# Last two expert steps: first weights ahead of the second weights, and a combine between the last sums

## The chip, the cores and the metric

The kernel runs on one core of a Trainium2 chip. The metric is the device time of one execution in microseconds (us); lower is better. The time before is the median of three runs, and one further execution was taken with the hardware profiler on.

## What is computed

The reference is a two-layer transformer block on 256 tokens of width 1024, all in fp32. Each layer has four kinds of attention with gates (the token mixers), a layer norm, then a grouped mixture of experts and a second layer norm. Only the mixture of experts is touched here:

```python
N_EXPERTS = 32; N_GROUPS = 8; TOP_K = 2; D_EXPERT = 256

def grouped_moe(x, w_router, router_bias, w1, w3, w2):
    ...  # one group of 4 experts per token, the best two experts in it, gates that sum to 1
    def expert_block(args):
        xb, e = args
        hid = jax.nn.silu(xb @ w1[e]) * (xb @ w3[e])
        return hid @ w2[e]
    ...
    y = jnp.zeros((t, d), x.dtype).at[tok].add(ys[dest] * gate_sorted[:, None])

for l in range(DEPTH):
    ...
    ffn = grouped_moe(x, w_router, router_bias, moe_w1[l], moe_w3[l], moe_w2[l])
    x = layer_norm(DN_ALPHA * x + ffn, ln2_g[l], ln2_b[l])
```

Per layer an expert has 1024x256 floats of `w1`, as many of `w3` ("first weights", 2 MB in all) and 256x1024 floats of `w2` ("second weights", 1 MB). With 32 experts that is 96 MB per layer, every byte of which is read once.

## The kernel before

Each layer first runs the mixers (projections, attention, gates, `w_out`), then routes the tokens, then works through the experts in a loop over `q` from 0 to 7 (L1535). A step `q` takes four experts: `2q`, `2q+1` and the same plus 16. Steps 0 to 5 pass two experts at a time through the array, with up to 64 tokens for each. The last two steps, 6 and 7 (`QUADS`, L43), put all four experts side by side as column tiles of 32 tokens.

What a step of the last two issues on TensorE, in this order:

- `head4` (L1385): for each of 8 slices `j` of the contraction and for each of the four experts `t`, one product with the first weights of 512 columns (L1390). One such product is two MATMUL instructions in the trace. The four experts lie in different columns of the array and run together where their data is there together.
- `combine` of the step before (L1480): the one-hot matrix `oht` times the step's gated outputs `ys`, added into the four accumulators `acc`; 8 matmuls (L1488).
- `flip_key` (L1462) for the one-hot matrix of this step, then `flip` (L1405), which transposes the hidden values into `hT`. ScalarE copies `hT` out of PSUM (L1410).
- `tail` (L1419): 16 products with the second weights (L1440), by halves `c` of the contraction and halves `fh` of the output columns. With four experts the order is `c`=0 for both `fh`, then `c`=1 for both. After `c`=1 of an `fh`, `evac` (L1424) takes the sum out: ScalarE L1430, then VectorE L1431.

After step 7 the last `combine` follows, then the statistics and the layer norm (`stats` L1635, `norm2` L1647). In layer 0 they lead into the next layer, in layer 1 to the output. In layer 1 `norm2` first loads its gain and offset, 512 KB each, into two of the four `b4` buffers (L1664); these are the buffers of step 6's `ys`, and so they come free with the combine of step 6.

TensorE's order is the order in which the code is written (`manual_schedule`, L1528); the other engines' orders follow from it through tile buffers and priorities.

The weights come by one queue, SyncE's, in the order of the list `loads` (L1048). A load of first weights (`load_head`, L1018) is two transfers of 512 KB for one expert's four slices of `w1` and `w3`; with four experts, all slices 0 to 3 come first, then all slices 4 to 7. A load of second weights is one transfer of 1 MB (`load_out`, L1025), and in step 7 two of 512 KB by `c`, all `c`=0 first (`load_out4`, L1039). Each transfer on the queue waits until the one eight places ahead of it has landed, since eight semaphores go round.

Weights land in 20 buffers of 1 MB (`SLOTS`, L41), taken in turn by `mslot` (L995). A buffer is free again when the products that read its contents 20 loads earlier have run. `release` (L1067) sets how many loads the program issues ahead.

`keep_warm` (L304) issues n fp32 products of 128x256 on the identity (L308), whose results nobody reads.

Of the kernel before, what the change touches and what calls it, by code (L numbers as in the profile page):

```python
# [10 lines left out]
F32 = mybir.dt.float32  # L11
# [35 lines left out]
NW3 = 5  # L47
NE_ = 4
# [54 lines left out]
def build(ctx, tc, I, consts, out, dbg=None, layers=L):  # L103
# [270 lines left out]
    for l in range(layers):  # L374
# [24 lines left out]
        with ExitStack() as mst:  # L399
# [649 lines left out]
            for q in range(NQ):  # L1049
                for s in range(2):  # L1050
                    a13s[q, s], a2s[q, s] = [{}, {}], [[], []]
                    if q not in QUADS:
                        loads += [partial(load_head, q, s, h) for h in range(4)]
                if q in QUADS:
                    loads += [partial(load_head, q, s, h) for h0 in (0, 2) for h in (h0, h0 + 1) for s in range(2)]
                if q == NQ - 1:
                    loads += [partial(load_out4, q, c, s, i) for c in range(2) for s in range(2) for i in range(2)]
                else:
                    loads += [partial(load_out, q, s, i) for s in range(2) for i in range(2) if q or s]

# [6 lines left out]
            def release(n):  # L1067
                cnt[1] += n
                load_ahead(cnt[1] + len(SLOTS))
# [271 lines left out]
        with ExitStack() as ost:  # L1341
# [77 lines left out]
            def tail(passes, gcol, out, final=None, between=None):  # L1419
# [14 lines left out]
                for s, (hT, tiles) in enumerate(passes):  # L1434
                    end = s == len(passes) - 1
                    four = len(tiles) == 4
                    for a, b in ((0, 0), (0, 1), (1, 0), (1, 1)):
                        fh, c = (b, a) if four else (a, b)
                        for r0, n, a2 in tiles:
                            pe.matmul(pys[fh][r0:r0 + n, :], hT[:, c, r0:r0 + n], a2[c][:, fh * 512:fh * 512 + 512],  # L1440
                                      start=(s == 0 and c == 0), stop=(end and c == 1), skip_group_check=True,
                                      tile_position=(0, r0) if four else None)
# [82 lines left out]

            xgs = {0: a8((8, G))}
            prev = None
            with tc.manual_schedule(engines={mybir.EngineType.PE}):  # L1528
# [6 lines left out]
                for q in range(NQ):  # L1535
                    b, o = q // 2, q % 2 * 128
                    more = b + 1 < NQ // 2
                    ths = []
                    if q in QUADS:
                        a13q = [a13s.pop((q, s)) for s in range(2)]  # L1540
                        ph = head4(lambda j, t: xgs[b][:, j, o + 32 * t:o + 32 * t + 32],
                                   [a13q[t % 2][t // 2] for t in range(4)])
                        release(8)
                        with behind_counts(q):
                            ths.append(hidden(ph, misc(6)))
                    for s in range(2) if q not in QUADS else ():
                        if q == 0 and s:
                            for tb in range(2):
                                pe.transpose(pkt[0:NP, tb, :], keyP[:, tb, :], ident)
                            act.activation(keyT[0:NP], pkt[0:NP], AF.Copy)  # L1550
                        ph = head(lambda j, i: xgs[b][:, j, o + 64 * i:o + 64 * i + 64], a13s.pop((q, s)),
                                  None if q or s else ph0)
                        release(3 if q == 1 and s == 0 else 4)
                        with behind_counts(q):
                            ths.append(hidden(ph, mk[:, s, q:q + 1]))
                    if o and more:
                        xgs[b + 1] = a8((8, G))
                    if prev is not None:
                        combine(*prev, first=q == 1)
# [9 lines left out]
                    hTs = [flip(th) for th in ths]  # L1569
                    if o and more:  # L1570
                        gather(xgs[b + 1], ohs[b + 1], G)
                    final = q == NQ - 1
# [6 lines left out]
                    else:  # L1579
                        passes = [(hT, pair_tiles(a2)) for hT, a2 in zip(hTs, a2q)]  # L1580
                    ys = tail(passes, gcols[q % 2], partial(b4, (2, 512)),
                              final, next_pieces if final and l + 1 < layers else None)
# [155 lines left out]
```

## Time and profile before

| What | Value |
|---|---|
| time before, median of 3 runs | 985.3 us (981.02 to 986.99) |
| profiled execution, its own time | 982.18 us |
| its span, first to last instruction | 980.4 us |
| mean granted TensorE clock | 0.987 of full speed |
| TensorE busy | 937.5 us (96%) |
| VectorE, ScalarE, GpSimdE busy | 489.1 (50%), 400.3 (41%), 199.4 us (20%) |
| SyncE's transfers | 282.48 MB, 77.9% of the DMA engines' time |
| last two steps of layer 0, of layer 1 | about 441 to 483 us, about 924 to 966 us |

All stretches below are microseconds from the start of the profiled span. The span lies inside the execution's own time; 1.8 us lie around it. The 77.9% are an average: in the expert loops of both layers the DMA engines are full, in the mixers they are not.

### The profile page before, as it was taken

Reading aid. Unit: us, or ns where it says so; the run is one execution under the profiler, and the core shown is the slowest. Engines: PE = TensorE matmul, PEld = TensorE weight load, DVE = VectorE, ACT = ScalarE, POOL = GpSimd, SP = SyncE. Lnnn points to the kernel's source line nnn. Section 1 sums busy time; section 2 is a strip of 40 time slices with the busy share of each in tenths; the row PEclk is TensorE's granted clock in tenths of the full one; section 3 lists DMA queues with packets and bytes.
Section 4 is the critical chain, followed back from the end, with each engine's and each line's share of the span. In section 5 each row is a group of like instructions: output and inputs, shape, how many; then the busy total and the mean of one; then the engine's idle time right before and its main releaser. Section 6 shows DMA issues by size and latency. Waiting matters only on the chain.

```text
span 980.4 us, 16559 instructions
## 1 busy us (share of the span) xinstructions
PE 937.5 (96%) x6335; PEld 668.1 (68%) x6335; DVE 489.1 (50%) x1158; ACT 400.3 (41%) x856; POOL 199.4 (20%) x190
## 2 busy tenths in 40 slices
PE   8999999999999999998799999999999999999964
PEld 7989999999953434342397999989999443343421
DVE  4776767766661212121277666686686521121214
ACT  4755666665431212120164766666654111121101
POOL 5440123122020313100045201140220203130001
PEclk9999999999999999999999999999999999999998
DMA  9795454469779999999998444534897899999994
GB/s 283 238 282 169 132 173 130 152 230 413 294 259 392 407 414 412 414 408 407 370 289 246 132 146 154 172 130 164 292 410 251 285 416 409 410 408 414 407 408 188
DMA packets 122585, 287.08 MB, mean 293 GB/s; under 512 B 10526, under 2 KB 73764, under 8 KB 115844
## 3 DMA queue, kind: packets, MB, share of 16 engines
q1 hardware_dynamic: 121092, 282.48, 77.9%
q0 software_dynamic: 1264, 3.41, 1.6%
q8 instruction: 52, 0.85, 0.4%
q14 instruction: 33, 0.27, 0.1%
q10 hardware_dynamic: 144, 0.07, 0.0%
HBM read 284.55 MB, written 1.38 MB: 292 GB/s over the span
## 4 chain that ended last, share of the span: by engine, by line
PE 63%; DMA 19%; issue 9%; DVE 6%; ACT 2%; POOL 0%; SPq 0%; POOLq 0%; ACTq 0%; DVEq 0%
PE pj L466 13%; PE pj L468 12%; PE pj L467 12%; DMA w<-in_moe_w 10%; PE h L1381 9%; DMA xw<-in_moe_w 7%; PE y L1440 4%; PE po L601 2%; PE at L613 2%; DMA w<-in_w_in 2%; PE tp L592 1%; PE at L308 1%; DVE b L421 1%; PE acc L1488 1%; DVE big L1215 1%
## 5 line engine op out<-in xcount | busy, mean ns | idle before, releaser
L421 DVE TENSOR_TENSOR b<-w,b 128x512 fp32r<-128x512 f32 (+2 forms) x294 | 212.2, 737 | 102.4 <-ACT b L416 98.1
L416 ACT ACTIVATE b<-w 128x512 fp32r<-128x512 f32 (+2 forms) x294 | 179.8, 623 | 130.5 <-PE pj L468 103.4
L466 PE MATMUL pj<-big,b 128*128 128x256 f32 x736 | 214.8, 292 | 1.7 <-ACT b L416 0.7
L468 PE MATMUL pj<-big,b 128*128 128x256 f32 x736 | 210.1, 285 | 1.5 <-DVE b L421 1.5
L467 PE MATMUL pj<-big,b 128*128 128x256 f32 x736 | 209.9, 285 | 0.0
L466 PEld LDWEIGHTS pj<-big,b 128*128 128x128 f32 x736 | 142.5, 194 | 8.2 <-issue 4.1
L468 PEld LDWEIGHTS pj<-big,b 128*128 128x128 f32 x736 | 142.6, 194 | 2.6 <-DVE b L421 2.1
L467 PEld LDWEIGHTS pj<-big,b 128*128 128x128 f32 x736 | 142.8, 194 | 0.1
L1401 DVE SCALAR_TENSOR_TENSOR th<-th,h 128x256 f32<-128x256 f32 x28 | 11.8, 420 | 178.2 <-ACT th L1400 178.2
L1381 PE MATMUL h<-xw,a 128*64 128x512 f32 x384 | 99.0, 594 | 0.1
L1400 ACT ACTIVATE th<-h 128x256 f32<-128x256 f32 x28 | 10.7, 383 | 204.8 <-PE h L1381 152.7
L1381 PE MATMUL h<-w,a 128*64 128x512 f32 x272 | 84.2, 593 | 0.0
L1431 DVE SCALAR_TENSOR_TENSOR b<-y,gcol,b 128x512 fp32r<-128x512 f32 x30 | 22.5, 751 | 100.6 <-ACT b L1430 93.7
L1440 PE MATMUL y<-w,hT 128*64 128x512 f32 (+1 forms) x256 | 66.2, 595 | 3.0 <-ACT hT L1410 2.8
L1381 PEld LDWEIGHTS h<-xw,a 128*64 128x64 f32 x384 | 31.4, 137 | 53.4 <-issue 49.3
L561 POOL TENSOR_TENSOR R<-R,a 128x512 f32<-128x512 f32 x20 | 35.3, 1776 | 111.9 <-DVE a L556 106.3
L466 PE MATMUL pj<-b,big 128*128 128x256 f32 x192 | 55.9, 291 | 1.6 <-ACT b L416 1.3
L1430 ACT ACTIVATE b<-y,gcol 128x512 fp32r<-128x512 f32 x30 | 20.6, 687 | 86.0 <-PE y L1440 81.1
L468 PE MATMUL pj<-b,big 128*128 128x256 f32 x192 | 55.1, 287 | 0.1
L467 PE MATMUL pj<-b,big 128*128 128x256 f32 x192 | 54.6, 285 | 0.0
L1381 PEld LDWEIGHTS h<-w,a 128*64 128x64 f32 x272 | 26.5, 137 | 31.6 <-issue 31.0
L856 POOL TENSOR_SCALAR bias<-OH 128x384 f32<-128x384 f32 x16 | 20.8, 1306 | 123.0 <-DVE mn L576 115.1
(383 smaller groups left out, 1749.3 us busy)
## 6 DMA issues: line engine op xcount, KB each, us to landing
xw<-in_moe_w SPq DMA_DIRECT2D x124, 512.0 KB, 10.5
w<-in_moe_w SPq DMA_DIRECT2D x116, 512.0 KB, 10.3
w<-in_w_gate SPq DMA_DIRECT2D x32, 1024.0 KB, 5.6
w<-in_moe_w SPq DMA_DIRECT2D x24, 1024.0 KB, 11.4
w<-in_w_in SPq DMA_DIRECT2D x18, 1024.0 KB, 13.1
xw<-in_moe_w SPq DMA_DIRECT2D x18, 1024.0 KB, 13.8
w<-in_w_out SPq DMA_DIRECT2D x8, 1024.0 KB, 5.4
ohl<-in_moe_w SPq DMA_DIRECT2D x12, 512.0 KB, 10.2
```

The source lines that it names most:

```text
L416: last_split[0] = act.activation(h, v, AF.Copy).ins
L421: last_split[1] = dve.tensor_sub(lo, v, h.bitcast(F32)).ins
L466: pe.matmul(o, lh, rh, start=start, stop=False, skip_group_check=True)
L467: pe.matmul(o, lh, rl, start=False, stop=False, skip_group_check=True)
L468: return pe.matmul(o, ll, rh, start=False, stop=stop, skip_group_check=True).ins
L561: eng.tensor_tensor(merged[:, c:c + 2, :], merged[:, c:c + 2, :], tc_, op=OP.add)
L601: pe.matmul(po[64 * hh:64 * hh + 64, c0:c1], v[i], PT[:, 256 * i:256 * i + c1 - c0], start=(i == 0), stop=(i == 1), skip_group_check=True)
L856: pool.tensor_scalar(bs, mc["sw3"][:, 0:384], slope_sw[2 * hp + hh], None, op0=OP.mult)
L1381: pe.matmul(ph[64 * i:64 * i + 64], xs(j, i), a13[i][j], start=(j == 0), stop=(j == 7), skip_group_check=True)
L1430: act.activation(ys[:, 0, :], py, AF.Copy, scale=gcol)
L1431: lows.append(dve.scalar_tensor_tensor(ys[:, 1, :], py, gcol, ys[:, 0, :].bitcast(F32), op0=OP.mult, op1=OP.subtract).ins)
L1440: pe.matmul(pys[fh][r0:r0 + n, :], hT[:, c, r0:r0 + n], a2[c][:, fh * 512:fh * 512 + 512], start=(s == 0 and c == 0), stop=(end and c == 1 ...
```

## The change

The loop's order for the last two steps is changed in three places.

1. The list of loads: the first weights of step 6, then those of step 7, then the second weights of step 6, then those of step 7. Step 6's second weights now come as halves by `c` too (`load_out4` for both steps).
2. TensorE's order: `head4` of step 7 is issued within step 6, between the transposes and the output products of step 6. The code of a step's first products moves into a function `heads`.
3. In step 7, `combine` of step 6 moves from ahead of the keys to between the `c`=0 and the `c`=1 products (`mid`), with three `keep_warm` products behind it (`NW4`).

```diff
--- before.py
+++ after.py
@@ -45,6 +45,7 @@
 NW1 = 9
 NW2 = 2
 NW3 = 5
+NW4 = 3
 NE_ = 4
 ROUTE0 = (2, 7)
 JH = (slice(0, 4), slice(4, 8))
@@ -1053,10 +1054,10 @@
                         loads += [partial(load_head, q, s, h) for h in range(4)]
                 if q in QUADS:
                     loads += [partial(load_head, q, s, h) for h0 in (0, 2) for h in (h0, h0 + 1) for s in range(2)]
-                if q == NQ - 1:
-                    loads += [partial(load_out4, q, c, s, i) for c in range(2) for s in range(2) for i in range(2)]
                 else:
                     loads += [partial(load_out, q, s, i) for s in range(2) for i in range(2) if q or s]
+            for q in QUADS:
+                loads += [partial(load_out4, q, c, s, i) for c in range(2) for s in range(2) for i in range(2)]
 
             def load_ahead(n):
 
@@ -1416,7 +1417,8 @@
             def pair_tiles(a2):
                 return [(0, 64, a2[0]), (64, 64, a2[1])]
 
-            def tail(passes, gcol, out, final=None, between=None):
+            def tail(passes, gcol, out, final=None, between=None, mid=None):
+
 
                 pys = [op.tile([128, 512], F32, name="y") for _ in range(2)]
                 ys_ = [None, None]
@@ -1436,6 +1438,8 @@
                     four = len(tiles) == 4
                     for a, b in ((0, 0), (0, 1), (1, 0), (1, 1)):
                         fh, c = (b, a) if four else (a, b)
+                        if mid and (a, b) == (1, 0):
+                            mid()
                         for r0, n, a2 in tiles:
                             pe.matmul(pys[fh][r0:r0 + n, :], hT[:, c, r0:r0 + n], a2[c][:, fh * 512:fh * 512 + 512],
                                       start=(s == 0 and c == 0), stop=(end and c == 1), skip_group_check=True,
@@ -1523,6 +1527,30 @@
                     behind.enter_context(tc.issue_after(getattr(c_, "ins", c_)))
                 return behind
 
+            def heads(q):
+                xg, o = xgs[q // 2], q % 2 * 128
+                if q in QUADS:
+                    a13q = [a13s.pop((q, s)) for s in range(2)]
+                    ph = head4(lambda j, t: xg[:, j, o + 32 * t:o + 32 * t + 32], [a13q[t % 2][t // 2] for t in range(4)])
+                    release(8)
+                    with behind_counts(q):
+                        return [hidden(ph, misc(6))]
+                ths = []
+                for s in range(2):
+                    if q == 0 and s:
+                        for tb in range(2):
+                            pe.transpose(pkt[0:NP, tb, :], keyP[:, tb, :], ident)
+                        act.activation(keyT[0:NP], pkt[0:NP], AF.Copy)
+                    ph = head(lambda j, i: xg[:, j, o + 64 * i:o + 64 * i + 64], a13s.pop((q, s)), None if q or s else ph0)
+                    release(3 if q == 1 and s == 0 else 4)
+                    with behind_counts(q):
+                        ths.append(hidden(ph, mk[:, s, q:q + 1]))
+                return ths
+
+            def combine_last():
+
+                keep_warm(op.tile([128, S], F32, name="h"), NW4, combine(*prev))
+
             xgs = {0: a8((8, G))}
             prev = None
             with tc.manual_schedule(engines={mybir.EngineType.PE}):
@@ -1535,27 +1563,12 @@
                 for q in range(NQ):
                     b, o = q // 2, q % 2 * 128
                     more = b + 1 < NQ // 2
-                    ths = []
-                    if q in QUADS:
-                        a13q = [a13s.pop((q, s)) for s in range(2)]
-                        ph = head4(lambda j, t: xgs[b][:, j, o + 32 * t:o + 32 * t + 32],
-                                   [a13q[t % 2][t // 2] for t in range(4)])
-                        release(8)
-                        with behind_counts(q):
-                            ths.append(hidden(ph, misc(6)))
-                    for s in range(2) if q not in QUADS else ():
-                        if q == 0 and s:
-                            for tb in range(2):
-                                pe.transpose(pkt[0:NP, tb, :], keyP[:, tb, :], ident)
-                            act.activation(keyT[0:NP], pkt[0:NP], AF.Copy)
-                        ph = head(lambda j, i: xgs[b][:, j, o + 64 * i:o + 64 * i + 64], a13s.pop((q, s)),
-                                  None if q or s else ph0)
-                        release(3 if q == 1 and s == 0 else 4)
-                        with behind_counts(q):
-                            ths.append(hidden(ph, mk[:, s, q:q + 1]))
+                    final = q == NQ - 1
+                    if not final:
+                        ths = heads(q)
                     if o and more:
                         xgs[b + 1] = a8((8, G))
-                    if prev is not None:
+                    if prev is not None and not final:
                         combine(*prev, first=q == 1)
                     if 2 <= q < 6:
                         xres = halves(q % 2, q // 4)
@@ -1567,9 +1580,10 @@
                             with ExitStack() if q else tc.issue_after(routed):
                                 ohs[b + 1], _ = onehot(b + 1)
                     hTs = [flip(th) for th in ths]
+                    if q == NQ - 2:
+                        ths = heads(NQ - 1)
                     if o and more:
                         gather(xgs[b + 1], ohs[b + 1], G)
-                    final = q == NQ - 1
                     if final and l + 1 < layers:
                         next_slots = list(mixer_slots(l + 1))
                         ahead = [slot(next_slots[0])]
@@ -1579,7 +1593,7 @@
                     else:
                         passes = [(hT, pair_tiles(a2)) for hT, a2 in zip(hTs, a2q)]
                     ys = tail(passes, gcols[q % 2], partial(b4, (2, 512)),
-                              final, next_pieces if final and l + 1 < layers else None)
+                              final, next_pieces if final and l + 1 < layers else None, combine_last if final else None)
                     release(4 if q else 2)
                     prev = (ys, oht)
                     if 2 <= q < 6:
```

SyncE's queue in layer 0, from the last loads of step 6's first weights on (L1007 first weights; L1036 and L1045 second weights; `xw`, `w`, `R`, `X` are buffers; 128x1024 is 512 KB, 128x2048 is 1 MB), before:

```order
L1007 DMA w<-in_moe_w 128x1024 x6
L1036 DMA w<-in_moe_w 128x2048
L1036 DMA R<-in_moe_w 128x2048
L1036 DMA X<-in_moe_w 128x2048
L1036 DMA xw<-in_moe_w 128x2048
L1007 DMA xw<-in_moe_w 128x1024 x14
L1007 DMA w<-in_moe_w 128x1024 x2
L1588 TENSOR_LOAD cmi
L1588 ISA x2
L1045 DMA w<-in_moe_w 128x1024 x8
L323 DMA w<-in_w_in 128x4x416 x2
```

The same place now (L1008 and L1046 are the lines of the same loads):

```order
L1008 DMA w<-in_moe_w 128x1024 x8
L1008 DMA R<-in_moe_w 128x1024 x2
L1008 DMA X<-in_moe_w 128x1024 x2
L1008 DMA xw<-in_moe_w 128x1024 x10
L1046 DMA xw<-in_moe_w 128x1024 x3
L1046 DMA w<-in_moe_w 128x1024
L1046 DMA xw<-in_moe_w 128x1024 x3
L1046 DMA w<-in_moe_w 128x1024
L1602 TENSOR_LOAD cmi
L1602 ISA x2
L1046 DMA w<-in_moe_w 128x1024 x8
```

The 16 transfers of step 7's first weights moved ahead of step 6's second weights, which are now eight transfers instead of four. The last eight transfers, step 7's second weights, stand where they stood.

TensorE's end of step 7 in layer 0 (L1390 first products, L1488 combine, L1466 keys, L1408 transposes, L1440 output products), before:

```order
L1390 MATMUL h<-xw,a_4448 32x512 x3
L1390 MATMUL h<-w,a_4448 32x512
L1488 MATMUL acc_3576<-b_4668,oht 128x512 x2
L1488 MATMUL acc_3578<-b_4668,oht 128x512 x2
L1488 MATMUL acc_3577<-b_4675,oht 128x512 x2
L1488 MATMUL acc_3579<-b_4675,oht 128x512 x2
L1466 LDWEIGHTS idb
L1466 MATMUL y<-keyT,idb 64x256
L1466 LDWEIGHTS idb
L1466 MATMUL y<-keyT,idb 64x256
L1408 MATMUL h<-K,th 128x128 x2
L1440 MATMUL y<-w,hT 32x512 x16
```

The same place now (L1409 transposes, L1444 output products, L1492 and L1488 combines, L309 `keep_warm`):

```order
L1409 MATMUL h<-K,th 128x128 x2
L1444 MATMUL y<-w,hT 32x512 x8
L1492 MATMUL acc_3576<-b_4709,oht 128x512 x2
L1492 MATMUL acc_3578<-b_4709,oht 128x512 x2
L1492 MATMUL acc_3577<-b_4716,oht 128x512 x2
L1492 MATMUL acc_3579<-b_4716,oht 128x512 x2
L309 MATMUL h<-K 128x256 x3
L1444 MATMUL y<-w,hT 32x512 x8
L1492 MATMUL acc_3576<-b_4757,oht 128x512 x2
L1492 MATMUL acc_3578<-b_4757,oht 128x512 x2
L1488 MATMUL acc_3577<-b_4770,oht 128x512
L1488 MATMUL acc_3579<-b_4770,oht 128x512
```

The 16 output products of step 7 are cut in two, and the combine of step 6 and three `keep_warm` products stand in the cut. The first products of step 7 stand further up, ahead of the output products of step 6. Both layers read alike.

## Rows read from the trace of the kernel before

**Rows 1.** Busy time by stretch, layer 1; first row names the columns.

```profile
core 0: us, PE busy (x) PEld busy (x) DVE busy (x) ACT busy (x) POOL busy (x), PEclk, DMA share, GB/s
920.00:930.00 10.00, 10.00 (x76) 3.15 (x76) 1.50 (x2) 1.37 (x2) 0.00 (x0) 1.00 1.00 410
940.00:950.00 10.00, 5.66 (x32) 1.39 (x32) 0.25 (x1) 0.00 (x0) 0.00 (x0) 1.00 1.02 406
950.00:960.00 10.00, 7.23 (x40) 2.90 (x40) 1.33 (x3) 0.40 (x2) 0.00 (x0) 1.00 1.03 409
```

**Rows 2.** Chain that ended last, end of layer 1: start, duration (us), what.

```profile
943.32 10.22 DMA w<-in_moe_w
...
953.56 10.19 DMA w<-in_moe_w
...
963.79 1.06 PE y L1440 x5
```

**Rows 3.** TensorE in order of time, end of layer 1: start, us, what, count.

```profile
957.20 2.10 PE L1488 MATMUL acc<-b,oht 128*128 128x512 f32 x8
959.23 0.29 PE L1466 MATMUL y<-keyT,idb 16*64 16x256 bf16 x2
...
960.42 3.17 PE L1440 MATMUL y<-w,hT 128*32 128x512 f32 x22 [0.53 <-ACT hT L1410]
963.79 1.90 PE L1440 MATMUL y<-w,hT 128*32 128x512 f32 x10 [0.20 <-DMA w<-in_moe_w]
```

**Rows 4.** SyncE queue in order of time, layer 0, second weights of step 7.

```profile
461.50 9.79 SPq L1045 DMA_DIRECT2D w<-in_moe_w  x8
```

**Rows 5.** All 16 transfers of line 1045: issue to landing.

```profile
DMA to landing us min/median/max: 10.2/10.2/10.8
```

**Rows 6.** TensorE in order of time, end of layer 0.

```profile
471.08 1.07 PE L1390 MATMUL h<-xw,a 128*32 128x512 f32 x3
...
471.93 1.07 PE L1390 MATMUL h<-xw,a 128*32 128x512 f32 x3
...
474.32 0.60 PE L1390 MATMUL h<-xw,a 128*32 128x512 f32 x3
...
474.75 0.60 PE L1390 MATMUL h<-xw,a 128*32 128x512 f32 x3
...
479.36 3.82 PE L1440 MATMUL y<-w,hT 128*32 128x512 f32 x32 [0.53 <-ACT hT L1410]
```

**Rows 7.** Busy time by stretch, layer 0; the clock is the figure behind POOL.

```profile
470.00:475.00 5.00, 3.92 (x24) 1.15 (x25) 0.00 (x0) 0.00 (x0) 0.00 (x0) 0.66 1.03 417
```

**Rows 8.** SyncE queue in order of time, layer 1.

```profile
913.23 0.33 SPq L1036 DMA_DIRECT2D w<-in_moe_w  x1
...
918.52 22.28 SPq L1007 DMA_DIRECT2D xw<-in_moe_w  x14
...
944.94 8.94 SPq L1045 DMA_DIRECT2D w<-in_moe_w  x8
958.46 0.33 SPq L1664 DMA_DIRECT2D b<-in_ln_g  x1
```

**Rows 9.** TensorE in order of time, layer 1, what follows step 5's products.

```profile
909.80 2.10 PE L1488 MATMUL acc<-b,oht 128*128 128x512 f32 x8
...
923.59 0.73 PE L1512 MATMUL acc<-b,idr 128*128 128x512 f32 x2
```

**Rows 10.** The `keep_warm` products of layer 0 in order of time.

```profile
488.05 2.40 PE L308 MATMUL y<-K 128*128 128x256 f32 x10 [0.94 <-DVEq L1702]
```

**Rows 11.** ScalarE, then VectorE, in order of time, layer 1.

```profile
937.84 0.69 ACT L1430 ACTIVATE b<-y,gcol 128x512 fp32r<-128x512 f32 x1 [2.90 <-PE y L1440]
...
938.56 0.75 DVE L1431 SCALAR_TENSOR_TENSOR b<-y,gcol,b 128x512 fp32r<-128x512 f32 x1 [4.03 <-ACT b L1430]
...
970.31 1.40 DVE L1671 SCALAR_TENSOR_TENSOR R<-acc,bmv,b 128x512 f32<-128x512 f32 x2
```

**Rows 12.** DMA issues, end of layer 1: size of one, median us to landing.

```profile
out<-X SPq DMA_DIRECT2D x4, 256.0 KB, 2.3
```

## The prediction

> **What bounds the kernel now.** I read the busy time by stretch first. In the last two expert steps of layer 1 the reader is to see two columns: the DMA share stays at 1.00 to 1.03 with 406 to 410 GB/s, while TensorE is busy for only 5.66 of 10 us and then 7.23 of 10 [rows 1]. So the weights set the pace there, not the products. The chain of waits says the same: it runs along weight transfers up to the last one, issued at 953.56, which lands 10.19 us later at 963.75, and only then through five output products (1.06 us) into the end [rows 2]. Eight transfers are in flight, so one of 512 KB lands every 10.2 / 8 = 1.28 us.
>
> TensorE in order of time shows how close the two are. In step 7 of layer 1 it starts the output products at 960.42, gets through 22 of the 32 instructions and waits 0.20 us for the last weights; the ten that remain take 1.90 us and end at 965.69 [rows 3]. In layer 0 the eight second-weight transfers go out from 461.50 on for 9.79 us; the last begins its 0.33 us at 470.96, and with 10.2 us to landing [rows 4, 5, 8] its weights are there at 481.2 (an estimate; with the longest, 10.8, at 481.8). The output products ran from 479.36 to 483.18 [rows 6], and 481.2 plus the same 1.9 us is 483.1. So both layers end with the weight stream plus 1.9 us.
>
> **The change part by part.** *First products of step 7 moved up.* What no longer stands between the last first weights and step 7's output products is the rest of these products, a combine (2.1 us in [rows 3]) and, for part of the wait, keys and transposes. That work ended in time for the last second weights already: gain 0. What is late next is what was late before, the last transfer. In layer 0 two groups of first products came 0.85 us apart at a granted clock of 0.66 of full speed in that stretch, and later 0.43 apart [rows 6, 7], so the engine was at the lower of its two levels (1.2 GHz) after waiting for weights; even so its output products met the end of the stream. A faster engine there gains nothing in the profiled execution.
>
> *Loads in another order.* The bytes are the same and the last eight transfers are the same, so the stream ends when it did if no buffer is late. Step 7's first weights now follow at 913.23, where step 6's second weights stood [rows 8]. Their buffers held step 5's first weights, whose products were over at 909.80; step 6's second weights go, some 16 × 1.28 us later (933.7), into buffers that step 5's output products left at 923.59 [rows 9]. Both are 3 us or more early: 0. The four 1 MB transfers become eight of 512 KB. The stretches in which 512 KB transfers landed moved 406 and 409 GB/s, that with the 1 MB ones 410 [rows 1]; 4.2 MB at 406 instead of 410 is 0.1 us a layer. The other end: a 256 KB transfer of the output, alone, takes 2.3 us to landing [rows 12], of which 0.6 us are data at 410 GB/s; four more transfers that each showed 1.7 us would cost 6.8 us a layer. With eight in flight the nearest row is the full stream, so I take 0.
>
> The Trainium skill speaks against this part: "DMA: Bandwidth & Descriptors", under Bandwidth, advises batching transfers to at least 1 MiB, and its fit under Anatomy of one DMA (2.0 us plus the bytes, for the queue that GpSimd issues) would price two halves instead of one whole at 2.0 us more, an estimate of 16 us for the eight pairs of both layers. By that rule the sum would be 16 us worse; by the rows, where halves run at 406 to 409 GB/s, nothing.
>
> *New waits.* The keys of step 7 use the PSUM buffers that step 6's output sums must leave first; before, the combine ahead of them covered this. Behind the waiting instruction are the transposes and all output products. Step 6's last half lands 8 × 1.28 us ahead of the end, at 953.5; its products end 1.9 us later, the first of the two sums one group (0.86 us) before that, at 954.6, and 0.69 + 0.75 us of ScalarE and VectorE [rows 11] put its evacuation at 956.0. Keys to first output product took 960.42 - 959.23 = 1.2 us [rows 3]: ready at 957.2. The first halves of step 7's second weights land by 963.75 - 4 × 1.28 = 958.6. Covered by 1.4 us: 0.
>
> *Combine and keep_warm between the sums.* This is what I charge. After the first halves have landed at 958.6, ten instructions (1.9 us) finish `c`=0, at 960.6. The combine adds 959.23 - 957.20 = 2.0: 962.6. Three `keep_warm` products are six instructions; ten took 2.40 us [rows 10], so 1.44: 964.05. The last weights are there at 963.75. Then the eight products of `c`=1 take the 1.9 us of two groups (before, the same time went to the last product of one group and the four of the next): end at 965.95 against 965.69, 0.26 later. In layer 0, from 481.2, the same steps give 483.4 against 483.18: 0.2. Below nothing: the warm products may keep the clock up, which in layer 0 had cost 0.4 us for each of three groups, 1.2 us in all [rows 6]. Above: the lower clock, in a rival below. I take +0.45 for both layers.
>
> *Gain and offset of the last norm.* Their loads waited for step 6's combine and went out at 958.46 [rows 8]; now they go at about 961.6 and 962.6. VectorE needs the first at 970.31 [rows 11]. Behind the stream, which ends at 963.75, two more of 512 KB are there by 963.75 + 2.6 = 966.3: 0. If they took the 10.2 us of a full queue, the first would be 1.5 us late; I keep that for the range.
>
> **The sum.** 0 + 0 + 0 + 0.45 + 0 on the profiled execution's own 982.18 is 982.6. That execution lies 3.1 us under the median of the runs, 985.3, so I forecast 985.3 + 0.45, about 985.7 us.
>
> **The rivals.**
>
> *A clock that was low more often (faster).* The 3.1 us by which the median lies above the profiled execution may be executions in which TensorE stayed at its lower level past 473.6 and step 7's chain came in after the weights. The moved products would take just that out: 985.3 - 3.1 = 982.2. For it: the low stretch in layer 0 [rows 6, 7]. Against it: in layer 1, with the same waits, the clock was full [rows 1], and in layer 0 the delay was hidden.
>
> *Combine and warm products at the low clock (slower).* Place: between the `c`=0 and `c`=1 products of step 7. Their work, 1.9 + 2.05 + 1.44 = 5.4 us, stands in a window of 4 × 1.28 = 5.1 us between the two landings, so from the first slow matmul every delay counts in full. At the lower level groups came 0.85 instead of 0.43 apart [rows 6], so 5.4 us become 10.7: 5.3 us more in a layer, 991.0 for one layer and 996.3 for both. For it: the products of step 6 and 7 now trickle behind transfers for 20 us ahead of that place. Against it: a single product (two instructions, 0.43 + 0.60 = 1.03 us by [rows 6]) per 1.28 us leaves shorter gaps than the first products had, which wait for pairs of transfers, 2.56 us apart, and the clock was full through these in layer 1 [rows 1].
>
> The Trainium skill has the rule for this in "TensorE: Matmul & The Clock Gate", HAM oscillation: bursts of matmuls with waits for DMA between them fall back to the half clock again and again. By it both layers would pay; the rows show one layer of two doing so.
>
> *Smaller transfers thin the stream (slower).* Four more transfers a layer at 1.7 us each: 985.3 + 13.6 = 998.9. Against it: the rows of full rate above.
>
> **How the numbers follow.** A difference of about 1%, 9.9 us, is what a measurement of this kernel can tell from no change. Chances: forecast 0.62, low clock removed 0.20, low clock in the new place 0.13 (one layer 0.09, both 0.04), smaller transfers 0.02, a cause that I do not see on the faster side 0.03. Slower by over 1% are both layers at low clock and the thin stream, 0.04 + 0.02 = 0.06; faster by over 1% only the unseen, 0.03; within 1% the rest, 0.91. The range reaches down to the low clock removed less the 1.2 us of the warm products, 981.0, and up to one layer of the slower rival, 991.0; it leaves out under 0.1. The likeliest case alone lies between 984.5 (the warm products gain 1.2) and 987.4 (0.2 for thinner transfers and 1.5 for a late gain besides the 0.45).
>
> **What would show it.** In the changed profile the last second weights of layer 1 should land within 0.5 us of 963.75, with the DMA share at 1.0 from 920 on; the first products of step 7 should be done by about 947; TensorE should be in the combine or `keep_warm`, or just through, when the last weights land; the products after them should end at 965.5 to 966.3. Wrong would be: last weights landing earlier or later by over 1 us, a clock under 1.00 in the last 6 us ahead of the last sums, output products that begin `c`=1 over 1 us after the landing, or VectorE waiting for the gain.

## The result and the profile after

The changed kernel takes 987.19 us (median of 15 runs, 985.96 to 993.63); the kernel before 982.59 us (15 runs, 979.48 to 986.99). The ratio is 1.006, with a 95% interval of 1.004 to 1.0079: slower by 0.6%, some 4.6 us. That is inside the range and within 1%, as forecast, but ten times the 0.45 us that the sum charged. The forecast of 985.7 us is only 1.5 us off because the 985.3 us it starts from, a median of 3 runs, lies 2.7 us above the 982.59 of the 15. The profiled execution took 987.19 us, its span 985.4 us against 980.4 before.

The queue of SyncE shows where the 5.0 us lie. First the changed kernel: the transfers into `ohl`, which belong to step 6's first weights in both kernels, then the end of the second weights, in layer 0 and in layer 1, and the load of the gain.

```profile
421.14 1.57 SPq L1008 DMA_DIRECT2D ohl<-in_moe_w  x2
...
463.68 11.41 SPq L1046 DMA_DIRECT2D w<-in_moe_w  x9
...
905.69 1.55 SPq L1008 DMA_DIRECT2D ohl<-in_moe_w  x2
...
947.63 10.83 SPq L1046 DMA_DIRECT2D w<-in_moe_w  x9
966.62 0.33 SPq L1678 DMA_DIRECT2D b<-in_ln_g  x1
```

The transfers into `ohl` in the kernel before:

```profile
420.47 1.56 SPq L1007 DMA_DIRECT2D ohl<-in_moe_w  x2
...
902.95 1.56 SPq L1007 DMA_DIRECT2D ohl<-in_moe_w  x2
```

At these transfers of layer 0 the kernel is 0.67 us later than before. The last second weights go out at 463.68 + 11.41 - 0.33 = 474.76 against 470.96 [rows 4]: 3.80 later, so the stretch loses 3.1 us. In layer 1 it starts 2.74 us late (some 1.1 us came back in between, where no code differs) and issues its last weights at 947.63 + 10.83 - 0.33 = 958.13 against 953.56 [rows 2]: 4.57 later, so that stretch loses 1.8 us. The rest, some 0.4 us, lies behind the last landing.

Not all of this is the new order's. The two lists are alike up to the transfer below, the first of step 7's first weights in the changed kernel and the first of step 6's second weights before:

```profile
432.46 1.53 SPq L1008 DMA_DIRECT2D w<-in_moe_w  x2
```

```profile
430.68 0.33 SPq L1036 DMA_DIRECT2D w<-in_moe_w  x1
```

Here layer 0 is 1.78 us late already: 1.1 of its 3.1 us were lost ahead of any difference, while the first halves of step 6 landed (353 GB/s in 424 to 428 us against 379 before). With one profile of the kernel before, it can't be told whether that part is chance. The new order itself loses 2.0 us in layer 0, and in layer 1, where the first transfer that differs is 2.68 us late (915.91 against 913.23 [rows 8]), 1.9 us.

Why the weights are late stands in the busy time by stretch. The changed kernel, columns as in [rows 1]; the last figure is GB/s, ahead of it the DMA share:

```profile
440.00:450.00 10.00, 10.00 (x77) 3.61 (x74) 2.24 (x4) 1.07 (x2) 0.00 (x0) 1.00 1.02 345
450.00:460.00 10.00, 7.22 (x47) 2.32 (x45) 0.80 (x3) 0.38 (x1) 0.00 (x0) 1.00 1.03 413
460.00:470.00 10.00, 7.22 (x38) 2.18 (x42) 0.00 (x0) 0.00 (x0) 0.00 (x0) 0.66 1.02 367
...
440.00:475.00 35.00, 27.70 (x176) 8.82 (x176) 3.94 (x9) 1.84 (x4) 0.00 (x0) 0.90 1.02 381
...
930.00:940.00 10.00, 10.00 (x83) 4.70 (x77) 1.70 (x5) 0.77 (x2) 0.00 (x0) 1.00 1.01 368
940.00:950.00 10.00, 5.51 (x24) 1.13 (x22) 0.00 (x0) 0.00 (x0) 0.00 (x0) 0.85 1.03 398
...
924.00:958.00 34.00, 27.73 (x178) 9.11 (x174) 4.11 (x9) 2.52 (x5) 0.00 (x0) 0.95 1.02 392
```

The same two long stretches of the kernel before, and two short ones in between:

```profile
440.00:475.00 35.00, 27.64 (x178) 8.86 (x177) 3.96 (x9) 2.83 (x5) 0.00 (x0) 0.90 1.02 404
...
460.00:470.00 10.00, 7.18 (x32) 1.84 (x32) 0.00 (x0) 0.00 (x0) 0.00 (x0) 0.83 1.03 398
464.00:468.00 4.00, 2.44 (x14) 0.43 (x6) 0.00 (x0) 0.00 (x0) 0.00 (x0) 1.00 1.04 377
...
924.00:958.00 34.00, 25.95 (x181) 8.58 (x180) 4.24 (x9) 2.95 (x6) 0.00 (x0) 1.00 1.02 412
```

The reader is to see that the DMA share is 1.01 to 1.04 everywhere and the bytes per time are not alike: 381 against 404 GB/s in layer 0 (35 x 23 / 404 = 2.0 us), 392 against 412 in layer 1 (34 x 20 / 412 = 1.7 us). The engines were never idle; their packets took longer. The share of busy time cannot tell a full stream from a slow one, only the GB/s beside it can. All transfers of line 1046 together (step 6's second weights included) took, from issue to landing, against 10.2/10.2/10.8 for step 7's alone in [rows 5]:

```profile
DMA to landing us min/median/max: 10.2/10.4/11.6
```

The end of layer 1, first the chain of waits:

```profile
953.10 10.37 DMA w<-in_moe_w
...
963.52 1.90 PE y L1444 x10
965.42 2.05 PE acc L1492 x8
967.47 1.29 PE h L309 x6
968.76 1.12 PE y L1444 x8
```

Then TensorE in order of time:

```profile
947.75 4.52 PE L1391 MATMUL h<-xw,a 128*32 128x512 f32 x25 [1.70 <-DMA xw<-in_moe_w]
...
960.77 0.29 PE L1470 MATMUL y<-keyT,idb 16*64 16x256 bf16 x2 [0.70 <-DVE b L1433]
...
968.69 1.92 PE L1444 MATMUL y<-w,hT 128*32 128x512 f32 x16
```

Where [rows 2] went from the last transfer straight into output products, the chain here takes the transfer of step 7's last first half (landing at 963.47), then `c`=0, combine, `keep_warm`, `c`=1. With 10.2 us to landing the last weights are there at 968.3, the products of `c`=1 begin at 968.7 and end at 970.61 (before 965.69). In layer 0 the same products, against [rows 6]:

```profile
485.08 1.92 PE L1444 MATMUL y<-w,hT 128*32 128x512 f32 x16
```

They end at 487.00, 3.82 us after those of before, and their last weights went out 3.80 us later.

### The profile page after: what moved, and what is told of

The parts are those of the page before. It is cut to its first block, busy times and chain, and to the rows that moved or that the text cites. A ratio compares the mean times of both kernels' runs of the same rounds, so it can differ in the third digit from the quotient of the medians.

```text
span 985.4 us, 16595 instructions
## 1 busy us (share of the span) xinstructions
PE 940.7 (95%) x6347; PEld 669.0 (68%) x6347; DVE 488.9 (50%) x1158; ACT 400.3 (41%) x856; POOL 201.6 (20%) x190
## 4 chain that ended last, share of the span: by engine, by line
PE 64%; DMA 17%; issue 10%; DVE 5%; ACT 2%; SPq 0%; POOL 0%; POOLq 0%; ACTq 0%; DVEq 0%
PE pj L467 12%; PE pj L469 12%; PE pj L468 12%; PE h L1382 10%; DMA w<-in_moe_w 9%; DMA xw<-in_moe_w 6%; PE y L1444 5%; PE po L602 2%; DMA w<-in_w_in 2%; PE at L614 1%; PE acc L1492 1%; PE tp L593 1%; DVE b L422 1%; DMA R<-in_moe_w 1%; PE at L309 1%
## 5 line engine op out<-in xcount | busy, mean ns | idle before, releaser
L1444 PE MATMUL y<-w,hT 128*64 128x512 f32 (+1 forms) x256 | 67.7, 596 | 2.8 <-ACT hT L1411 1.7
L1444 PE MATMUL y<-xw,hT 128*64 128x512 f32 (+1 forms) x176 | 46.1, 599 | 3.0 <-DMA xw<-in_moe_w 3.0
## 6 DMA issues: line engine op xcount, KB each, us to landing
w<-in_moe_w SPq DMA_DIRECT2D x120, 512.0 KB, 10.2
```

## The experiments

Each was measured beside the kernel before, which took 985.16 us beside the first four, 984.09 us beside the next four and 985.11 us beside the last; each ratio is to that time. The letters A, B, C, P and Q are names of theories in the expectations. A blames the halves of step 6's second weights, B the order of the loads, C the new place of the combine.

### The old order with halves

The kernel before; step 6's second weights come as eight halves.

```diff
-                if q == NQ - 1:
+                if q in QUADS:
                     loads += [partial(load_out4, q, c, s, i) for c in range(2) for s in range(2) for i in range(2)]
```

> The kernel before, with step 6's second weights loaded as eight halves of 512 KB instead of four wholes; nothing else. Theory A (smaller transfers thin the weight stream): most of the 4.6 us is back, +3 to +5 us against the kernel before, and the last second weights of layer 0 are issued 2 us or more later after the first of step 6's than the 40.3 us of before. Theory B (the order of the loads thins it): within 1 us of the kernel before. Theory C (the combine and keep_warm between the sums cost it): within 1 us of the kernel before.

Measured: 986.89 us, ratio 1.0021 [1.0004, 1.0038]. Halves alone cost 0.2%, some 2 us: less than A had (3 to 5 us) and more than B and C had (within 1 us). Nor did A's sign come: in layer 0 the last second weights go out 40.9 us after the first of step 6's, not 2 us or more beyond 40.3. The stream is thin where step 7's first halves follow them, here in layer 1:

```profile
940.00:950.00 10.00, 5.58 (x30) 1.30 (x26) 1.50 (x2) 1.38 (x2) 0.00 (x0) 0.79 1.02 363
```

### The new order with whole transfers

The changed kernel; step 6's second weights come as four transfers of 1 MB in their new place.

```diff
-            for q in QUADS:
-                loads += [partial(load_out4, q, c, s, i) for c in range(2) for s in range(2) for i in range(2)]
+            loads += [partial(load_out, NQ - 2, s, i) for s in range(2) for i in range(2)]
+            loads += [partial(load_out4, NQ - 1, c, s, i) for c in range(2) for s in range(2) for i in range(2)]
```

> The changed kernel, with step 6's second weights as four whole transfers of 1 MB at their new place. Theory A: back to about the kernel before plus the 0.45 us charged in the prediction (983 us where before is 982.6). Theory B: as the changed kernel, +4 to +5 us. Theory C: as the changed kernel, +4 to +5 us; the last second weights would land when they do in the kernel before.

Measured: 989.5 us, ratio 1.0054 [1.0035, 1.0073]: as slow as the changed kernel. A falls: the order costs without the halves, and the thin stretches stand where step 7's first weights follow step 6's:

```profile
440.00:450.00 10.00, 10.00 (x77) 3.46 (x74) 2.09 (x4) 1.26 (x3) 0.00 (x0) 1.00 1.02 353
...
930.00:940.00 10.00, 10.00 (x83) 4.71 (x79) 1.71 (x5) 0.77 (x2) 0.00 (x0) 1.00 1.02 374
```

### The combine at its old place

The changed kernel with the combine of step 6 ahead of step 7's keys again, without the three `keep_warm` products.

```diff
-                    if prev is not None and not final:
+                    if prev is not None:
...
-                              final, next_pieces if final and l + 1 < layers else None, combine_last if final else None)
+                              final, next_pieces if final and l + 1 < layers else None)
```

> The changed kernel, with the combine of step 6 back ahead of the keys of step 7 and without the three keep_warm products; loads and first products as changed. Theory A and B: 0.2 to 0.6 us faster than the changed kernel, the last weights landing as late as there. Theory C: 3 us or more faster than the changed kernel, close to the kernel before.

Measured: 988.68 us, ratio 1.0039 [1.0023, 1.0054]; the changed kernel again, measured beside it and shown below: 1.0043 [1.0022, 1.0064]. Taking the combine and the warm products out of the way gains nothing that can be measured: C falls. The stream is as thin as in the changed kernel:

```profile
440.00:450.00 10.00, 10.00 (x78) 2.85 (x74) 1.50 (x2) 1.38 (x2) 0.00 (x0) 1.00 1.02 358
...
930.00:940.00 10.00, 10.00 (x82) 4.09 (x78) 1.71 (x5) 0.77 (x2) 0.00 (x0) 1.00 0.99 343
```

### The changed kernel again

> The changed kernel once more, for a second trace. If the thin stretches of the weight stream belong to the change, they stand in both layers again, where step 7's first weights land (about 442 to 452 and 928 to 936 us), and the last weights of each layer land 3 us or more later after the first of step 6's second-weight places than in the kernel before. If they are chance, they stand elsewhere or are gone and the time falls with them.

Measured: 988.28 us, ratio 1.0043 [1.0022, 1.0064]. The thin stretches stand at the same places as in the first profile (345 and 368 GB/s there), so they belong to the program and not to one execution. B is left, with some 2 us for halves in the old order that it did not have:

```profile
440.00:450.00 10.00, 10.00 (x78) 3.55 (x75) 2.25 (x4) 1.11 (x3) 0.00 (x0) 1.00 1.02 342
...
930.00:940.00 10.00, 10.00 (x84) 4.07 (x80) 1.71 (x5) 0.77 (x2) 0.00 (x0) 1.00 1.02 358
```

So the order thins the stream; why? A partition's piece of an expert's `w1`, `w3` or `w2` is 8 KB in memory. A half transfer reads 4 KB of each, and in the last two steps all four experts' first halves come before all their second halves, so that for first weights eight transfers in flight can all read the first half of every 8 KB. Before, four 1 MB transfers, which read whole 8 KB, lay between step 6's runs and step 7's. The theory P: the stream is thin where all that is in flight reads the same half.

### Mixed halves

The changed kernel; for the experts from 16 on (`s`=1) the second half is loaded and used first, in both steps, so that halves alternate in the queue. Sizes, bytes and buffers of the transfers and the order of the experts in the queue stay, and so does the place of the combine. Each sum is the same, in another order of its terms.

```diff
-                                            h // 2 * 4, 4))
+                                            (h // 2 ^ (s if q in QUADS else 0)) * 4, 4))
...
-                last_load[0] = nc.sync.dma_start(a2s[q, s][i][c], src[:, c]).ins
+                last_load[0] = nc.sync.dma_start(a2s[q, s][i][c ^ s], src[:, c ^ s]).ins
...
-                        pe.matmul(ph[32 * t:32 * t + 32], xs(j, t), a13[t][j], start=(j == 0), stop=(j == 7),
+                        k = j ^ 4 * (t % 2)
+                        pe.matmul(ph[32 * t:32 * t + 32], xs(k, t), a13[t][k], start=(j == 0), stop=(j == 7),
...
+                            k = c ^ r0 // 32 % 2 if four else c
```

In the output products `k` then stands for `c` in `hT` and `a2`.

> The changed kernel; of the experts 16 and up in the last two steps, each weight's second half is loaded and used first, so that first and second halves of rows (4 KB at the same offset of every 8 KB in memory) alternate in the stream instead of coming in runs of eight or sixteen. Theory P (the stream is thin where all transfers in flight read the same half of every 8 KB): the slow packets go, 20 us windows move 405 GB/s or more, the last weights come 3 to 5 us earlier than in the changed kernel, and the time falls by 3 to 5 us. Theory Q (what thins it is only how many 512 KB transfers follow one another, or which engine works beside them): as the changed kernel, within 1 us.

Measured: 983.37 us, ratio 0.9976 [0.9956, 0.9997]. The loss is gone and turns into a gain: from 1.0043 to 0.9976 is some 6.6 us, more than the 3 to 5 that P had. Every stretch is full:

```profile
440.00:450.00 10.00, 10.00 (x81) 4.14 (x80) 2.23 (x5) 0.52 (x2) 0.00 (x0) 1.00 1.03 408
...
460.00:470.00 10.00, 8.27 (x52) 2.02 (x49) 0.90 (x2) 0.38 (x1) 0.00 (x0) 0.86 1.03 411
...
930.00:940.00 10.00, 8.46 (x57) 3.63 (x54) 1.70 (x5) 0.77 (x2) 0.00 (x0) 1.00 1.03 409
940.00:950.00 10.00, 7.67 (x46) 1.86 (x44) 0.90 (x2) 0.38 (x1) 0.00 (x0) 1.00 1.03 409
```

At the end of layer 1 TensorE shows what the prediction had as a rival, the low clock around the moved combine:

```profile
957.45 3.47 PE L1446 MATMUL y<-w,hT 128*32 128x512 f32 x10 [0.23 <-DMA w<-in_moe_w]
960.85 2.19 PE L1494 MATMUL acc<-b,oht 128*128 128x512 f32 x8
962.88 1.46 PE L309 MATMUL h<-K 128*128 128x256 f32 x6
964.27 1.92 PE L1446 MATMUL y<-w,hT 128*32 128x512 f32 x16
```

Ten products took 3.47 us instead of 1.90; the granted clock of 956 to 961 us is 0.66 of full speed, so most of this stretch lies at the lower level, 1.2 GHz. Combine and warm products ran at full speed again. The weights were there at about 962.5 (issue 942.08 + 10.56 - 0.33 = 952.31, and 10.2 to landing), so `c`=1 began 1.8 us late instead of the 0.3 forecast: 1.5 us for one layer, where the rival had 5.3. The profiles of mixed halves in the first weights alone and of second halves first for all, both below, show the same at this place; their ten products of layer 1:

```profile
958.29 3.53 PE L1445 MATMUL y<-w,hT 128*32 128x512 f32 x10 [0.26 <-DMA w<-in_moe_w]
```

```profile
971.48 3.60 PE L1446 MATMUL y<-w,hT 128*32 128x512 f32 x10 [0.22 <-DMA w<-in_moe_w]
```

### Mixed halves in the kernel before

The same edits in the kernel before.

> The kernel before with the same alternation of halves in its last two steps. Theory P: its own thin stretches (376 and 377 GB/s of 4 us in layer 0, 382 in layer 1) go, 1 to 2 us faster than the kernel before. Theory Q: as the kernel before, within 1 us.

Measured: 980.94 us, ratio 0.9966 [0.9948, 0.9984]: faster than before by 0.3%. P had 1 to 2 us; it is some 3. The kernel before had thin stretches of its own (398 GB/s in 460 to 470 us), which now are full:

```profile
450.00:460.00 10.00, 9.47 (x76) 3.95 (x68) 2.10 (x6) 1.62 (x4) 0.00 (x0) 1.00 1.02 409
460.00:470.00 10.00, 5.45 (x35) 1.39 (x32) 1.11 (x2) 0.52 (x1) 0.00 (x0) 1.00 1.02 408
```

### Mixed halves in the first weights alone

The changed kernel with the edits of `load_head` and `head4` only; the second weights keep all first halves first.

> The changed kernel with the alternation in the first weights alone; second weights as changed. Theory P: two thirds of what e5 gives, since the thin stretch of the second weights of step 6 stays. Theory Q: as the changed kernel, within 1 us.

Measured: 981.98 us, ratio 0.9972 [0.9953, 0.999]: the same as with both mixed, where P had two thirds of it. To break up the long runs of first weights is enough. It also settles a rival: the two transfers of a load fill the two halves of one buffer (`load13`), mixed or not, so where the data goes did not change here, only which half of the 8 KB is read when:

```profile
440.00:450.00 10.00, 10.00 (x78) 2.85 (x74) 1.50 (x2) 1.38 (x2) 0.00 (x0) 1.00 1.03 409
...
930.00:940.00 10.00, 9.15 (x68) 3.72 (x60) 1.70 (x5) 0.77 (x2) 0.00 (x0) 1.00 1.02 408
```

### Mixed halves and the combine at its old place

The edits of the third and the fifth experiment together.

> The changed kernel with the alternation of halves, the combine of step 6 ahead of the keys of step 7 and no keep_warm products there. Theory P: as e5 less 0.2 to 0.6 us. Theory Q: as the changed kernel, within 1 us.

Measured: 980.88 us, ratio 0.9964 [0.9948, 0.998]. It beats both kernels and is as fast as the kernel before with mixed halves, within their intervals; so the order of the change gains nothing that can be measured once the stream is full. Against mixed halves with the moved combine (983.37 us) it is 2.5 us lower where 0.2 to 0.6 were expected, but the intervals of the two overlap. The chain at the end of layer 1 has the form of [rows 2] again, with transfers of 10.2 us throughout:

```profile
941.36 10.21 DMA w<-in_moe_w
...
951.59 10.21 DMA w<-in_moe_w
...
961.85 1.06 PE y L1446 x5
```

### Second halves first for all

Left to tell: is it that all in flight read the same half, or are first halves slow to read? The changed kernel, as with mixed halves but with the second half first for all four experts; the products take them in that order.

```diff
-                                            (h // 2 ^ (s if q in QUADS else 0)) * 4, 4))
+                                            (h // 2 ^ (1 if q in QUADS else 0)) * 4, 4))
...
-                last_load[0] = nc.sync.dma_start(a2s[q, s][i][c ^ s], src[:, c ^ s]).ins
+                last_load[0] = nc.sync.dma_start(a2s[q, s][i][c ^ 1], src[:, c ^ 1]).ins
```

> The changed kernel; in the last two steps every transfer of a half reads the second 4 KB of the 8 KB rows first and the first 4 KB later, for all four experts, and the products take them in that order. So the runs of eight transfers that read the same half remain, and only which half comes first is swapped. If what makes the stream thin is that all transfers in flight read the same half, whichever it is, the time is that of the changed kernel, 987 to 989 us (ratio 1.003 to 1.007), and the thin stretches stay at the same places, about 444 to 452, 460 to 468 and 928 to 936 us, with 320 to 375 GB/s. If it is the first half that is slow to read, the thin stretches move by eight transfers, 10 us, to about 452 to 460, 468 to 474 and 936 to 944 us, with the time still near that of the changed kernel. If the slowness comes from the two halves being read in ascending order, it goes, with 408 to 411 GB/s throughout and 981 to 984 us.

Measured: 992.4 us (5 runs), ratio 1.0068 [1.0045, 1.0091]: slow like the changed kernel. Its ratio lies in the 1.003 to 1.007 expected, its median 3 us above the upper end. In this execution step 7's first weights (the transfers into `X`) go out 2.4 us later than in the changed kernel in layer 0 (439.97 against 437.53) and 5.8 us later in layer 1 (926.80 against 921.03). The thin stretches are later by that and not by 10 us more. They stand, as in the changed kernel, at the end of step 7's run of halves that are read first, which now are the second (448 to 454 and 936 to 942 us), and in layer 0 at the end of the run behind it (464 to 470 us):

```profile
448.00:454.00 6.00, 6.00 (x51) 2.28 (x43) 0.70 (x2) 0.39 (x1) 0.00 (x0) 1.00 1.02 336
464.00:470.00 6.00, 2.84 (x14) 0.73 (x18) 0.00 (x0) 0.00 (x0) 0.00 (x0) 0.70 0.99 348
936.00:942.00 6.00, 6.00 (x47) 3.00 (x42) 1.71 (x5) 0.39 (x1) 0.00 (x0) 1.00 1.00 326
```

So it isn't the first half that is slow, nor the rising order of the two halves, nor the order of the products: it is the run of transfers that read one and the same half.

## Why the prediction was right or wrong

The time lies in the range, but that is luck as far as the mechanism goes: the loss came from a part that the sum put at 0. "A difference of about 1%" as what can be told from no change was too coarse as well: the interval is 0.2% to either side, and 0.6% stands clear of it.

**What bounds the kernel: right.** Both layers end with the weight stream plus the last products, and every kernel here is as late as its last weights, but for the 1.5 us of the low clock in three of the profiles.

**Loads in another order: wrong.** The step that failed is "so I take 0". The working asked whether buffers are late and whether transfers are smaller. The buffers were not late, and size was not the cause: whole transfers in the new order were as slow, and halves that alternate ran at 408 to 411 GB/s. What the step did not ask is which addresses the eight transfers in flight read at one time. In place of 0 the new order lost 2.0 us in layer 0 and 1.9 us in layer 1, inside the bound of 0.1 to 6.8 us a layer, but by a mechanism that stood in no term and in no rival. The rows for the 0 came from layer 1 of one execution, and in layer 0 the kernel before shows 398 GB/s in 460 to 470 us and 377 in 464 to 468, where step 7's first weights land: the sign was there and was not read.

The Trainium skill ("DMA: Bandwidth & Descriptors") spoke against this part: its rule under Bandwidth is to batch to at least 1 MiB, and its fit under Anatomy of one DMA gave the estimate of 16 us more. The runs don't bear it out as a matter of size: halves alone cost some 2 us, and with the same sizes the ratio goes from 1.0043 to 0.9976 by swapping halves.

**Combine and keep_warm between the sums: right in the changed kernel.** The charge was 0.26 us in layer 1; `c`=1 begins 0.4 us after the landing and the end has 0.35 us beyond the shift of the weights. In layer 0, 0.02 instead of 0.2. By the runs, the old place gains nothing that can be told from zero (1.0039 beside 1.0043, and 0.9964 beside 0.9976).

**New wait of the keys: right.** They waited 0.70 us for VectorE and were through at 961.06, so the first output products behind them were at work when the last first half landed at 963.47.

**First products moved up: half right.** Gain 0, as said; but they were done at about 952.3 and not by 947, since their weights were late as well.

**Gain and offset: right.** The load goes out at 966.62, and VectorE takes the value at 975.32 without a wait:

```profile
975.25 0.16 DVE L1671 TENSOR_SCALAR mr<-bmv 128x2 f32<-128x2 f32 x1
975.32 1.40 DVE L1685 SCALAR_TENSOR_TENSOR R<-acc,bmv,b 128x512 f32<-128x512 f32 x2
```

**What would show it.** "Last second weights within 0.5 us of 963.75" failed: 968.3. "DMA share at 1.0 from 920 on" held and told nothing, since a slow packet is busy too.

**The rivals.** Low clock removed: the gain did not come, and in layer 0 the clock in 460 to 470 us is 0.66. Low clock in the new place: not in the two profiles of the changed kernel, whose ten last products of `c`=0 in layer 1 took 1.90 and 1.91 us, but in three others with the combine there (mixed halves, mixed halves in the first weights alone, second halves first), at some 1.5 us each (3.47 to 3.60 us for the ten). What sets these apart was not tried. The Trainium skill's rule ("TensorE: Matmul & The Clock Gate", HAM oscillation) thus showed in some executions, in one layer, and at under a third of the price that the rival gave it. Smaller transfers thin the stream: it named the right place and the wrong cause; its 998.9 lies outside all that was measured.

## What to carry to other kernels

Read the GB/s beside the DMA share: a queue can be full and slow. Where a matrix is loaded in halves of its rows, let the transfers that are in flight together read different halves; in this kernel that was worth 0.3% without any other change, and without it a new order of the same loads cost 0.4 to 0.6%. When loads change places, ask which of them will now be in flight together, and not only whether their buffers are free.

## What the runs showed of the hardware

Transfers of 512 KB, 128 rows of 4 KB at a distance of 8 KB, ran at 408 to 411 GB/s with halves mixed and, in the two profiles of the changed kernel, at 342 to 368 over 10 us where runs of them read the same half, with the DMA share at 1.01 to 1.03 in both. The slow place is the end of such a run: in layer 0 of the changed kernel 444 to 452 us, where the last of step 7's first halves land, and 460 to 468 us, where the last of its second halves and the first transfers behind them land; in layer 1 only the first of the two (929 to 936 us). From the trace's DMA packets, those of the weight queue (4 KB and more) that took over 0.25 us per 4 KB, counted from 40 us ahead of the last second weights' issue to 10 us behind it:

```
kernel                               layer 0   layer 1
before                                    49        40
changed                                  162       104
changed, again                           171       132
old order with halves                     71       109
new order with whole transfers           129       141
combine at old place                     164        92
second halves first for all              191       201
changed, mixed halves                      8         6
before, mixed halves                      10         4
changed, mixed in first weights           10        20
mixed halves, combine at old place        10         6
```

Where the stream is thin they are some 70 to 200 packets out of 4,000 to 5,000, and the middle packet takes 0.16 us per 4 KB in every kernel: a few long waits and not an even loss. What the slow ones took beyond 0.16 us per 4 KB, shared among 16 engines, is 2.8 and 1.8 us in the changed kernel and 0.9 and 0.6 us before: the difference is nearly all of the 2.0 us that the new order lost in layer 0, and two thirds of the 1.9 in layer 1. What in the memory makes them wait, and why the run of second halves goes mostly free in layer 1 and not in layer 0, was not tried and stays open. The kernel with second halves first lost more beside before than the changed one (7.3 us against 4.6 and 3.1), with intervals that overlap; its profile has further thin stretches in layer 1 (914 to 918 and 950 to 958 us, 337 to 362 GB/s over 4 us) and the low clock, and why is open too. The Trainium skill ("DMA: Bandwidth & Descriptors", Latency and other measured facts) tells of rows at large powers of two apart: copies made 103 GB/s with rows 4 or 8 MiB apart, 214 with the same 4 MiB padded by 4 KiB, and 207 at 512 KiB, the smallest pitch it has; it calls the cause an inference. No run here has such a pitch: the rows of this case are 8 KB apart.
